# A hybrid retention and sparse-attention layer: pairs of seven in the output projection, a new order in the block sums, idle matmuls ahead, tables spread out, last chunk by token tile

## Chip, core and metric

The kernel runs on one core of a Trainium2 chip. The metric is the device time of one execution in microseconds; the median of three runs of the kernel before is 1888.11 us.

## What is computed

One layer on 256 tokens of width 2048, all in 32-bit floating point: a gated feed-forward network (inner width 5632), a mixer of two halves (retention, and attention over the 64 best keys of an index score), and a second feed-forward network, each added to `x`.

```python
def swiglu(h, w_gate, w_up, w_down):
    return (jax.nn.silu(h @ w_gate) * (h @ w_up)) @ w_down
...
        x = x + 0.5 * swiglu(rmsnorm(x, ffn1_norm[l]), ffn1_w_gate[l], ffn1_w_up[l], ffn1_w_down[l])
        h = rmsnorm(x, mix_norm[l])
        proj = h @ w_in[l]
...
        x = x + jnp.concatenate([ro, ao], axis=-1) @ w_out[l]
        x = x + 0.5 * swiglu(rmsnorm(x, ffn2_norm[l]), ffn2_w_gate[l], ffn2_w_up[l], ffn2_w_down[l])
    return rmsnorm(x, final_norm)
```

## The kernel before

**Products.** Every 32-bit operand is split in two parts, `hi` (rounded by a copy on ScalarE) and `lo` (what is left, a subtraction on VectorE). A product is three matmuls: hi x hi, hi x lo, lo x hi. All have 128 rows of weights and 512 columns.

**Weights.** They come from memory once, 1 MB at a time for two k-tiles of 128 (a "pair"), into `raw` (three buffers), all from SyncE's queue. `split` cuts a pair into pieces of up to 1024 columns and makes `hi` (L269, ScalarE) and `lo` (L275, VectorE) of each; five buffers of each hold them, so a piece is made up to four pieces ahead of its matmuls (two for the first eleven).

**Chunks.** `wide` plans 1024 output columns by two token tiles of 128: 2 x 2 output blocks of 128x512. A pair of kind "C" has eight block products, 24 matmuls (L221). A pair of kind "S" gets the same result from seven products, 21 matmuls, of sums and differences of blocks. It needs four raw sums of the weights on VectorE (`less`, L261), four pieces (512 columns of one product's weights are new), and block sums of the left operand, which `blocks_of` makes (L296 to L306). The products add up in eight PSUM banks: four of output blocks (MAP_B) and four (M1, M5, M6, M7) that `sums_of` combines (L437) once the last pair of seven is done. `UP` names the kinds of the eight pairs of a chunk over the 2048 inputs, `DOWN` those over the hidden inputs. An up chunk is 22 pieces.

**Order.** Each engine runs its instructions in program order. The main loop does, for piece i: the splits up to four pieces ahead, the steps that fall due at i (`after(i, f)`), then the matmuls of i. So a step's instructions on VectorE and ScalarE stand between the `lo` and `hi` of pieces that are four ahead, and wait there for each other.

**A feed-forward network.** It runs in two parts of six and five up chunks, each followed by two down chunks. At the end of an up chunk `hidden` applies the gate (L517, L522). Two pieces or so into the next chunk each half of the result, 256 columns, is transposed on TensorE (`turn`, L529) for the down chunks: where `DOWN` has "S" for the pair it is copied to `b` (L533) and goes through `blocks_of`, where it has "C" it is split plainly (L537, L538). The first up chunk is `PLAIN` and stands in the banks of MAP_A; the others use `UP` and MAP_B. x comes transposed too (`in_xT`), and `x_for` (L288, L324) makes the left operand of each pair of it: pairs 0, 2 and 4 are "S".

**Around the mixer.** `tables` computes angles for the rotary factors in the first network's time on VectorE, steps L617 to L644, with one piece between steps (`yield 1`). The output projection is two chunks of `PLAIN`. `finish` (L581, L583) runs after the last matmul: squares, root of the mean, scaling, four outputs of 512 KB.

Of the kernel before, what the change touches and what calls it, by code (L numbers as in the profile page):

```python
# [19 lines left out]
P = 128  # L20
# [7 lines left out]

PLAIN = "CCCCCCCC"
UP = "SCSCSCCC"  # L30
# [19 lines left out]
def layer(ctx: ExitStack, tc: tile.TileContext, a: dict, out: bass.AP):  # L50
# [32 lines left out]
    MAP_A = {"11": "M7", "12": "M1", "21": "M6", "22": "M5"}  # L83
    MAP_B = {"11": "M2", "12": "M3", "21": "M4", "22": "M8"}
    turn = [0, 0]

    def pair():
        turn[0] += 1
        return [[bank["M1"], bank["M5"]], [bank["M6"], bank["M7"]]][turn[0] % 2]

    def small():
        turn[1] += 1
        return [bank["M2"], bank["M3"], bank["M4"], bank["M8"]][turn[1] % 4]
# [12 lines left out]

    now = [0]
# [66 lines left out]
    def wide(src, plan, left, cmap, x0=False):  # L174

        start = len(pieces)
        seen, last = {}, {}
        s_end = None

        def mm(i, off, a, m):  # L180

            for n, (u, v) in enumerate(((0, 0), (0, 1), (1, 0))):
                st = m not in seen
                seen[m] = 1
                e = [i, off, a, m, u, v, st, False]
                last[m] = e
                pieces[i]["mms"].append(e)

        for p, kind in enumerate(plan):
            loads.append([(0, block(src, 2 * p, 2 * p + 2, 1024))])  # L190
            if x0:
                loads[-1] = [lambda p=p: load_xT(p)] + [(o, loads[-1][0][1][:, o:o + n]) for o, n in
                                                        ([(0, 512), (512, 512), (1024, 1024)] if p == 0 else [(0, 2048)])]
            i = len(pieces)
            if kind == "C":
                tiles = [(0, 1024), (1024, 1024)]
                if x0 and p == 0:
# [6 lines left out]
            if kind == "C":  # L204
                for c in (1, 0):
                    for k in range(2):
                        off = 1024 * (1 - c) + 512 * k
                        j = max(j for j, (o, n) in enumerate(tiles) if o <= off)
                        for t in range(2):
                            mm(i + j, off - tiles[j][0], (t, k), cmap[f"{t + 1}{c + 1}"])  # L210
# [8 lines left out]
    def run_mms(p, hi, lo):  # L219
        for _, off, a, m, u, v, st, sp in p["mms"]:  # L220
            TE.matmul(bank[m], lhsT=p["left"](p["pair"], a)[u], rhs=(hi, lo)[v][:, off:off + 512], start=st, stop=sp)  # L221
# [28 lines left out]
    def split(i):  # L250
# [22 lines left out]
        elif k == 2:  # L273
            less(512, 1536, 1536)
# [17 lines left out]
    def blocks_of(v, sums, alone):  # L292
# [7 lines left out]
        S.activation(alone[:, :2, 0], v[:, :, 0], AF.Copy)  # L300
        S.activation(alone[:, 2, 0], v[:, 1, 1], AF.Copy, scale=-1.0)
        S.activation(sums[:, :, 0], f, AF.Copy)
        V.tensor_tensor(alone[:, :2, 1], v[:, :, 0], alone[:, :2, 0].bitcast(F32), op=OP.subtract)
        V.scalar_tensor_tensor(alone[:, 2, 1], v[:, 1, 1], -1.0, alone[:, 2, 0].bitcast(F32),
                               op0=OP.mult, op1=OP.subtract)
        V.tensor_tensor(sums[:, :, 1], f, sums[:, :, 0].bitcast(F32), op=OP.subtract)  # L306
        return sums, alone

    def s_block(pair, a):
        sums, alone = pair  # L310
        t, i = (sums, int(a[1]) - 1) if a[0] == "S" else (alone, ("A11", "A12", "A22").index(a))
# [97 lines left out]
    def rstd_tok(norm):  # L409
        v = new(tmp, [P, 2], F32, "sum_v", 1)  # L410
        s, k = squares[norm]
        V.tensor_reduce(v, s[:, :, :k[0]], axis=AX.X, op=OP.add)
        V.tensor_scalar(v, v, 1.0 / D, EPS, op0=OP.mult, op1=OP.add)
        r_tok[norm] = new(one, [P, 2], F32, f"r_tok{norm}")
        rsqrt(r_tok[norm], v, 2)
# [41 lines left out]
    def grow(d, scale, at, cmap, norm, done=None):  # L457
# [9 lines left out]
        def ready(c):  # L467
            for t in range(2):
                add_x(t, d, c, bank[cmap[f"{t + 1}{c + 1}"]], scale)

        if s_end is not None:
            after(s_end, early)
        after(half, lambda: ready(1))
# [9 lines left out]
    marks = {}  # L483

    def ffn(which, norm, next_norm, last):
        wgu, wd = a[f"wgu{which}"], [a[f"wd{which}{j}"] for j in range(2)]
        c = 0
        for part, n in enumerate(PARTS):
            hs = {}
            marks[which, part] = len(pieces)  # L490
            for cc in range(n):
                cmap = MAP_A if c == 0 else MAP_B
                start, s_end, half, end = wide(wgu[c], PLAIN if c == 0 else UP, left_of(xg if c == 0 else xs), cmap,
                                               c == 0 and which == 1)
# [638 lines left out]
```

## Time and profile before

| what | us |
|---|---|
| three runs | 1887.54, 1888.11, 1888.51 |
| profiled execution | 1887.65 |
| its span | 1885.8 |
| TensorE busy | 1856.2 (98%) |
| VectorE busy | 1625.8 (86%) |
| ScalarE busy | 1064.9 (56%) |

The span runs from the first to the last instruction that the profiler saw; the 1.85 us around it belong to the execution. Busy time of matmuls overlaps a little, as one is fed while the one before it drains. Rows give the start and the length of an operation in microseconds; behind it, in brackets, stands how long its engine was idle ahead of it, and what ended that.

### The profile page before, as it was taken

What the parts mean: (1) busy time and instruction counts of PE and PEld (TensorE: products, weight loads), DVE (VectorE), ACT (ScalarE), POOL (GpSimd) and SP (SyncE); (2) the same over time, 40 slices, a digit from 0 to 9 for tenths busy, and PEclk for the clock granted to TensorE, in tenths of its full rate; (3) what the DMA queues carried; (4) which work ended last, traced back from release to release, by engine and by line L of the source; (5) the groups of instructions that cost most, each with busy time, mean ns of one, the idle gap of its engine ahead of it and who ended that gap; (6) DMA issues with size and microseconds to landing.
All of it is one profiled execution on the core that took longest, in us unless ns stands there. A gap on an engine that the chain in (4) does not pass through costs nothing.

```text
span 1885.8 us, 22691 instructions
## 1 busy us (share of the span) xinstructions
PE 1856.2 (98%) x8624; PEld 1527.1 (81%) x8624; DVE 1625.8 (86%) x2076; ACT 1064.9 (56%) x1348; POOL 5.3 (0%) x14
## 2 busy tenths in 40 slices
PE   8999999999999999999999999999999999999997
PEld 6788888887888887988888888788888888888886
DVE  7899998889999997789865756799999889999997
ACT  7555655544555555656544555555555455555554
POOL 0000000000000000000000000000000000000000
PEclk9999999999999999999999999999999999999998
DMA  8544555545555454545534444545555555455454
GB/s 323 191 178 180 199 201 221 192 170 178 194 206 203 172 208 156 187 164 211 179 134 173 168 174 178 198 181 191 209 203 180 199 201 200 180 191 210 180 198 159
DMA packets 51309, 359.33 MB, mean 191 GB/s; under 512 B 5856, under 2 KB 5856, under 8 KB 8704
## 3 DMA queue, kind: packets, MB, share of 16 engines
q1 hardware_dynamic: 50400, 355.62, 51.6%
q8 instruction: 67, 1.10, 0.2%
q10 hardware_dynamic: 432, 1.08, 0.2%
q0 software_dynamic: 368, 1.19, 0.2%
q14 instruction: 42, 0.34, 0.1%
HBM read 355.76 MB, written 2.10 MB: 190 GB/s over the span
## 4 chain that ended last, share of the span: by engine, by line
PE 93%; DVE 5%; ACT 1%; issue 1%; DMA 0%; DVEq 0%; ACTq 0%
PE M L221 75%; PE M L145 8%; PE M L147 4%; DVE lo L275 2%; PE M L529 1%; PE M L163 1%; PE M L164 1%; PE M L162 1%; DVE raw L261 1%; DVE x L434 1%; ACT hi L269 1%; PE M L790 0%; DVE e L437 0%; PE M L838 0%; PE M L144 0%
## 5 line engine op out<-in xcount | busy, mean ns | idle before, releaser
L269 ACT ACTIVATE hi<-raw 128x1024 fp32r<-128x1024 f32 (+2 forms) x853 | 843.9, 1008 | 578.8 <-DVE raw L261 356.3
L275 DVE TENSOR_TENSOR lo<-raw,hi 128x1024 fp32r<-128x1024 f32 (+2 forms) x853 | 974.5, 1160 | 152.7 <-ACT hi L269 137.7
L221 PE MATMUL M<-hi,xg 128*128 128x512 f32 x2240 | 738.3, 396 | 1.4 <-DVE e L437 1.4
L221 PE MATMUL M<-hi,mid 128*128 128x512 f32 x1696 | 531.1, 392 | 8.2 <-ACT hi L269 7.8
L221 PEld LDWEIGHTS M<-hi,xg 128*128 128x128 f32 x2240 | 422.6, 189 | 99.5 <-DVE e L437 1.9
L221 PE MATMUL M<-lo,xg 128*128 128x512 f32 x1120 | 444.4, 397 | 2.3 <-DVE lo L275 2.1
L221 PEld LDWEIGHTS M<-hi,mid 128*128 128x128 f32 x1696 | 319.4, 188 | 75.9 <-ACT hi L269 7.8
L221 PE MATMUL M<-lo,mid 128*128 128x512 f32 x848 | 331.5, 391 | 0.1
L261 DVE TENSOR_TENSOR raw<-raw 128x512 f32<-128x512 f32 x368 | 254.7, 692 | 12.4
L221 PEld LDWEIGHTS M<-lo,xg 128*128 128x128 f32 x1120 | 211.4, 189 | 56.7 <-DVE lo L275 8.7
L145 PE MATMUL M<-xg,hi 128*128 128x512 f32 x688 | 245.2, 398 | 1.3 <-DVE xg L289 1.1
L221 PEld LDWEIGHTS M<-lo,mid 128*128 128x128 f32 x848 | 159.8, 188 | 34.6 <-DVE lo L275 1.8
L147 PE MATMUL M<-xg,lo 128*128 128x256 f32 x645 | 182.1, 282 | 0.0
L145 PEld LDWEIGHTS M<-xg,hi 128*128 128x128 f32 x688 | 128.3, 188 | 30.7 <-DVE xg L289 2.2
L221 PE MATMUL M<-hi,ext 128*128 128x512 f32 x360 | 142.4, 395 | 1.9 <-DVE e L522 1.7
L147 PEld LDWEIGHTS M<-xg,lo 128*128 128x128 f32 x645 | 121.4, 188 | 0.8
L221 PEld LDWEIGHTS M<-hi,ext 128*128 128x128 f32 x360 | 67.8, 188 | 18.9 <-DVE e L522 2.6
L221 PE MATMUL M<-lo,ext 128*128 128x512 f32 x180 | 71.2, 395 | 0.1
L437 DVE TENSOR_TENSOR s<-s,M 128x512 f32<-128x512 f32 x96 | 64.1, 682 | 2.2 <-PE M L221 1.2
L517 ACT ACTIVATE s<-s,r_tok 128x512 f32<-128x512 f32 x40 | 27.0, 718 | 54.6 <-DVE s L437 54.6
L221 PEld LDWEIGHTS M<-lo,ext 128*128 128x128 f32 x180 | 33.9, 188 | 8.3 <-DVE lo L275 0.5
L704 ACT ACTIVATE b<-e 64x512 f32<-64x512 f32 (+2 forms) x46 | 28.1, 612 | 19.5 <-DVE e L690 18.9
(173 smaller groups left out, 910.2 us busy)
## 6 DMA issues: line engine op xcount, KB each, us to landing
raw<-in_wgu SPq DMA_DIRECT2D x175, 1024.0 KB, 4.8
raw<-in_wd SPq DMA_DIRECT2D x88, 1024.0 KB, 4.8
raw<-in_w_out SPq DMA_DIRECT2D x16, 1024.0 KB, 4.8
raw<-in_w_iq SPq DMA_DIRECT2D x8, 1024.0 KB, 4.8
raw<-in_w_aq SPq DMA_DIRECT2D x8, 1024.0 KB, 4.8
raw<-in_w_rk SPq DMA_DIRECT2D x8, 1024.0 KB, 4.9
raw<-in_w_rq SPq DMA_DIRECT2D x8, 1024.0 KB, 4.8
raw<-in_w_rv SPq DMA_DIRECT2D x8, 1024.0 KB, 4.8
```

The lines of the kernel that those rows point to most:

```text
L145: TE.matmul(acc, lhsT=hi[:, c:c + P], rhs=r, start=st, stop=sp)
L147: TE.matmul(acc[:, T:], lhsT=lo[:, c:c + P], rhs=r[:, :T], start=False, stop=False)
L162: TE.matmul(o, lhsT=h, rhs=hi[:, i * n:(i + 1) * n], start=st, stop=False)
L163: TE.matmul(o, lhsT=h, rhs=lo[:, i * n:(i + 1) * n], start=False, stop=False)
L164: TE.matmul(o, lhsT=l, rhs=hi[:, i * n:(i + 1) * n], start=False, stop=sp)
L221: TE.matmul(bank[m], lhsT=p["left"](p["pair"], a)[u], rhs=(hi, lo)[v][:, off:off + 512], start=st, stop=sp)
L261: V.tensor_tensor(r[:, o:o + 512], r[:, a:a + 512], r[:, b:b + 512], op=OP.subtract)
L269: S.activation(hi[:, :p["n"]], raw, AF.Copy)
L275: V.tensor_tensor(lo[:, :p["n"]], raw, hi[:, :p["n"]].bitcast(F32), op=OP.subtract)
L437: V.tensor_tensor(o, a, b, op=OP.add)
L517: S.activation(s, g, AF.Silu, scale=r_tok[norm][:, t:t + 1])
L704: S.activation(b[p0:p0 + w], q[p1:p1 + w], AF.Copy)
```

## The change

- The output projection's first chunk uses `UP` (three pairs of seven), its second stays plain and uses the banks of OTHER. `left_pair` makes a left operand of either kind, for the mixer's results too.
- `UP` is now "CSCSCSCC", and `ORDER` lays the pairs out so that a chunk still runs S C S C S C C C. The pairs of x that are "S" are 1, 3 and 5; x's first pair is split plainly.
- `blocks_of` issues ScalarE's copy of the four sums ahead of that of the blocks that stand alone; the latter are four (of x three), in one copy and one subtraction; the sign of one block moves into the raw sums.
- The plain chunk of each network stands in the banks SUM, and its results are copied or gated from there.
- Fourteen idle matmuls of 128 columns stand ahead of all others.
- `tables` has three pieces between steps.
- In the last chunk the matmuls of the last two pairs are ordered by token tile; `finish` does all of a tile before the other, in pieces of 512 columns, with eight outputs of 256 KB; `gain_first` comes at the last three pieces instead of the last eight.
- The transposes of x around the second network use other banks (`turn_early`, `turn_late`).

```diff
+UP = "CSCSCSCC"
+ORDER = (1, 0, 3, 2, 5, 4, 6, 7)
 PLAIN = "CCCCCCCC"
-UP = "SCSCSCCC"
...
-    MAP_A = {"11": "M7", "12": "M1", "21": "M6", "22": "M5"}
-    MAP_B = {"11": "M2", "12": "M3", "21": "M4", "22": "M8"}
+    SUM = {"11": "M2", "12": "M3", "21": "M4", "22": "M8"}
+    OTHER = {"11": "M7", "12": "M1", "21": "M6", "22": "M5"}
...
+                            if tail and p >= len(plan) - 2:
+                                ending[t].append((i + j, off - tiles[j][0], p, (t, k), sums[f"{t + 1}{c + 1}"]))
+                                continue
+                            mm(i + j, off - tiles[j][0], (t, k), sums[f"{t + 1}{c + 1}"])
...
+        ending[1].sort(key=lambda e: e[4], reverse=True)
+        for t in range(2):
+            for i, off, p, a, m in ending[t]:
+                mm(i, off, a, m, i if t == 0 else len(pieces) - 1)
...
-            less(512, 1536, 1536)
+            less(1536, 512, 1536)
...
-        S.activation(alone[:, :2, 0], v[:, :, 0], AF.Copy)
-        S.activation(alone[:, 2, 0], v[:, 1, 1], AF.Copy, scale=-1.0)
+        vt = v.rearrange("p k t n -> p t k n")
         S.activation(sums[:, :, 0], f, AF.Copy)
-        V.tensor_tensor(alone[:, :2, 1], v[:, :, 0], alone[:, :2, 0].bitcast(F32), op=OP.subtract)
-        V.scalar_tensor_tensor(alone[:, 2, 1], v[:, 1, 1], -1.0, alone[:, 2, 0].bitcast(F32),
-                               op0=OP.mult, op1=OP.subtract)
+        if alone.shape[1] == 4:
+            a4 = alone.rearrange("p (t k) h n -> p t k h n", t=2)
+            S.activation(a4[:, :, :, 0], vt, AF.Copy)
+            V.tensor_tensor(a4[:, :, :, 1], vt, a4[:, :, :, 0].bitcast(F32), op=OP.subtract)
+        else:
+            for o, w in ((slice(0, 2), vt[:, 0]), (slice(2, 3), vt[:, 1, 1:2])):
+                S.activation(alone[:, o, 0], w, AF.Copy)
+                V.tensor_tensor(alone[:, o, 1], w, alone[:, o, 0].bitcast(F32), op=OP.subtract)
         V.tensor_tensor(sums[:, :, 1], f, sums[:, :, 0].bitcast(F32), op=OP.subtract)
...
+    def left_pair(kind, v, in_psum=True):
+
+        if kind == "S":
+            if in_psum:
+                f = half_k("b")
+                S.activation(f, v, AF.Copy)
+                v = f
+            return blocks_of(v, big(F32R, (P, 4, 2, P)), big(F32R, (P, 4, 2, P)))
+        t = big(F32R, (P, 2, 512))
+        S.activation(t[:, :, :T], v, AF.Copy)
+        V.tensor_tensor(t[:, :, T:], v, t[:, :, :T].bitcast(F32), op=OP.subtract)
+        return t
...
+                def ups(u=u, plain=plain):
                     for b in ("12", "22"):
-                        if b in u:
-                            full(b)
-
-                def hidden(u=u, full=full, cc=cc, part=part, hs=hs, cmap=cmap):
-                    ht, sil = [], []
+                        if plain:
+                            u[b] = new(tmp, [P, W], F32, "e", 3)
+                            S.activation(u[b], bank[SUM[b]], AF.Copy)
+                        else:
+                            tt(u[b], u[b], bank[SUM[b]])
...
+                    for b in ("11", "21"):
+                        t = int(b[0]) - 1
+                        if plain:
+                            u[b] = new(tmp, [P, W], F32, "s")
+                        else:
+                            tt(u[b], u[b], bank[SUM[b]])
+                        S.activation(u[b], bank[SUM[b]] if plain else u[b], AF.Silu, scale=r_tok[norm][:, t:t + 1])
+                    ht = [u["12"], u["22"]]
...
+            rstd_tok(3, slice(t, t + 1))
             r = r_tok[3][:, t:t + 1]
-            xs = [x[t][:, halves(c, 1024)] for c in range(2)]
-            S.activation(xs[0], xs[0], AF.Copy, scale=r)
-            V.scalar_tensor_tensor(xs[1], xs[1], r, last_gain[1], op0=OP.mult, op1=OP.mult)
-            for c in range(2):
-                nc.sync.dma_start(out[t][:, halves(c, 1024)], xs[c])
+            for c in range(4):
+                xs = x[t][:, halves(c)]
+                if c < 2:
+                    S.activation(xs, xs, AF.Copy, scale=r)
+                else:
+                    V.scalar_tensor_tensor(xs, xs, r, last_gain[1][:, halves(c - 2)], op0=OP.mult, op1=OP.mult)
+                nc.sync.dma_start(out[t][:, halves(c)], xs)
...
+    for _ in range(14):
+        TE.matmul(bank["M1"][:, :P], lhsT=ones, rhs=ones, start=True, stop=True)
...
-        yield 1
+        yield 3
...
-        cmap = (MAP_A, MAP_B)[d]
-        at = wide(a["w_out"][d], PLAIN, left_of(mix_in), cmap)
-        grow(d, 1.0, at, cmap, 2)
+        sums = OTHER if d else SUM
+        at = wide(a["w_out"][d], PLAIN if d else UP, left_of(mix_in), order=None if d else ORDER, sums=sums)
+        grow(d, 1.0, at, 2, sums=sums)
...
-    after(end - 8, gain_first)
+    after(end - 3, gain_first)
```

A turn for a pair of seven (523 us in the trace of before): ScalarE, from the copy out of PSUM (`b`) to the next weight piece's `hi`. `sq` holds the four sums, the `mid` after it is the sums' parts, that with `b` as its source the blocks that stand alone. Before:

```order
L533 ACTIVATE b_1448<-M_5_76 128x512
L300 ACTIVATE mid_1451<-b_1448 128x2x128
L301 ACTIVATE mid_1451<-b_1448 128x128
L302 ACTIVATE mid_1450<-sq_1452 128x4x128
L537 ACTIVATE mid_1467<-M_7_78 128x2x256
L269 ACTIVATE hi_1470<-raw_1381 128x1024
```

Two copies of alone blocks stand ahead of the copy of the sums. After, the same place on ScalarE:

```order
L329 ACTIVATE b_1460<-M_5_76 128x512
L312 ACTIVATE mid_1462<-sq_1464 128x4x128
L315 ACTIVATE mid_1463<-b_1460 128x4x128
L333 ACTIVATE mid_1477<-M_7_78 128x2x256
L280 ACTIVATE hi_1480<-raw_1393 128x1024
```

The copy of the sums now stands first, that of the alone blocks behind it. VectorE in the same turn, before:

```order
L299 TENSOR_TENSOR sq_1452<-b_1448,sq_1452 128x128
L303 TENSOR_TENSOR mid_1451<-b_1448,mid_1451 128x2x128
L304 SCALAR_TENSOR_TENSOR mid_1451<-b_1448,mid_1451 128x128
L306 TENSOR_TENSOR mid_1450<-sq_1452,mid_1450 128x4x128
L538 TENSOR_TENSOR mid_1467<-M_7_78,mid_1467 128x2x256
L275 TENSOR_TENSOR lo_1471<-raw_1381,hi_1470 128x1024
```

The residues of the alone blocks read what L300 and L301 wrote, that of the sums what L302 wrote. After, on VectorE:

```order
L310 TENSOR_TENSOR sq_1464<-b_1460,sq_1464 128x128
L316 TENSOR_TENSOR mid_1463<-b_1460,mid_1463 128x4x128
L321 TENSOR_TENSOR mid_1462<-sq_1464,mid_1462 128x4x128
L334 TENSOR_TENSOR mid_1477<-M_7_78,mid_1477 128x2x256
L286 TENSOR_TENSOR lo_1481<-raw_1393,hi_1480 128x1024
```

The alone residue is one operation, still first, and reads what ScalarE's second copy wrote. The program's start on ScalarE: `e` is a transposed pair of x, `xg` and `mid` its plain parts, `b` the copy for the sums, `ext` the alone blocks of x. Before:

```order
L288 ACTIVATE mid_114<-e_101,gains_72 128x256 x2
L324 ACTIVATE b_119<-e_101,gains_72 128x256 x2
L300 ACTIVATE ext_123<-b_119 128x2x128
L301 ACTIVATE ext_123<-b_119 128x128
L302 ACTIVATE xg_29_122<-sq_124 128x4x128
L269 ACTIVATE hi_135<-raw_100 128x512
L269 ACTIVATE hi_139<-raw_100 128x512
L269 ACTIVATE hi_143<-raw_100 128x1024
L288 ACTIVATE xg_40_157<-e_107,gains_72 128x256 x2
L269 ACTIVATE hi_162<-raw_106 128x1024
```

After:

```order
L299 ACTIVATE xg_27_128<-e_115,gains_72 128x256 x2
L280 ACTIVATE hi_133<-raw_114 128x512
L280 ACTIVATE hi_137<-raw_114 128x512
L280 ACTIVATE hi_141<-raw_114 128x1024
L299 ACTIVATE mid_155<-e_121,gains_72 128x256 x2
L357 ACTIVATE b_160<-e_121,gains_72 128x256 x2
L312 ACTIVATE xg_38_163<-sq_165 128x4x128
L319 ACTIVATE ext_164<-b_160 128x2x128
L319 ACTIVATE ext_164<-b_160 128x128
L280 ACTIVATE hi_176<-raw_120 128x1024
```

The block sums moved from ahead of the first pair's weights to ahead of the second pair's.

## Rows read from the trace of the kernel before

**Rows 1.** Part 1 of the page: busy time, share of the span, instructions.

```profile
PE 1856.2 (98%) x8624; PEld 1527.1 (81%) x8624; DVE 1625.8 (86%) x2076; ACT 1064.9 (56%) x1348; POOL 5.3 (0%) x14
```

**Rows 2.** Waits of TensorE: total us, times, longest.

```profile
PE M L221 <- ACT hi L269: 7.8, 1, 7.8
PE M L221 <- DVE lo L275: 2.1, 2, 1.8
```

**Rows 3.** Timeline of VectorE, 515 to 560 us: start, length, operation.

```profile
523.74 0.29 DVE L299 TENSOR_TENSOR sq<-b,sq 128x128 f32<-128x128 f32 x1
...
524.73 0.69 DVE L306 TENSOR_TENSOR mid<-sq,mid 128x512 fp32r<-128x512 f32 x1 [0.16 <-ACT mid L302]
525.34 0.68 DVE L538 TENSOR_TENSOR mid<-M,mid 128x512 fp32r<-128x512 f32 x1
526.16 1.23 DVE L275 TENSOR_TENSOR lo<-raw,hi 128x1024 fp32r<-128x1024 f32 x1
...
538.93 1.42 DVE L522 SCALAR_TENSOR_TENSOR e<-e,r_tok,s 128x512 f32<-128x512 f32 x2 [0.20 <-ACT s L517]
540.49 3.50 DVE L275 TENSOR_TENSOR lo<-raw,hi 128x1024 fp32r<-128x1024 f32 x3
```

**Rows 4.** Timeline of ScalarE, 515 to 560 us.

```profile
524.06 0.63 ACT L302 ACTIVATE mid<-sq 128x512 fp32r<-128x512 f32 x1 [0.44 <-DVE sq L299]
524.60 0.58 ACT L537 ACTIVATE mid<-M 128x512 fp32r<-128x512 f32 x1
```

**Rows 5.** Timeline of TensorE, 540.5 to 543.2 us.

```profile
541.21 0.40 PE L221 MATMUL M<-hi,ext 128*128 128x512 f32 x1
541.44 0.40 PE L221 MATMUL M<-hi,xg 128*128 128x512 f32 x1
541.77 0.50 PE L221 MATMUL M<-lo,xg 128*128 128x512 f32 x1
```

**Rows 6.** Groups by line and form: count, busy us, mean ns, idle ahead.

```profile
L306 DVE TENSOR_TENSOR mid<-sq,mid 128x512 fp32r<-128x512 f32 x16 | 11.1, 693 | 2.6 <-ACT mid L302 2.6
```

**Rows 7.** Timeline of TensorE, 54 to 57 us.

```profile
54.51 0.39 PE L221 MATMUL M<-hi,xg 128*128 128x512 f32 x1
55.76 0.50 PE L221 MATMUL M<-hi,ext 128*128 128x512 f32 x1 [0.86 <-DVE e L522]
```

**Rows 8.** Stretches: length, busy us (instructions) of PE, PEld, DVE, ACT, POOL; clock; DMA.

```profile
410.00:453.60 43.60, 40.01 (x162) 30.84 (x161) 42.91 (x58) 18.93 (x22) 0.00 (x0) 0.96 0.47 161
...
497.20:540.80 43.60, 43.60 (x193) 35.08 (x192) 41.49 (x53) 25.18 (x31) 0.00 (x0) 1.00 0.52 192
```

**Rows 9.** Stretches in the output projection, the same columns.

```profile
1080.00:1100.00 20.00, 20.00 (x90) 16.57 (x89) 9.42 (x9) 8.26 (x8) 0.00 (x0) 1.00 0.50 167
1100.00:1120.00 20.00, 20.00 (x90) 16.57 (x89) 11.94 (x12) 10.06 (x14) 0.00 (x0) 1.00 0.57 206
```

**Rows 10.** Groups by line: the first and the last of the tables' twelve.

```profile
L617 DVE CAST mid<-mid 128x256 f32<-128x256 int32 x1 | 0.3, 286 | 0.0
...
L644 DVE TENSOR_SCALAR mid<-mid 128x1024 f32<-128x1024 f32 x1 | 0.7, 683 | 0.0
```

**Rows 11.** Timelines of the start.

```profile
9.24 1.05 PE L221 MATMUL M<-hi,mid 128*128 128x512 f32 x2
9.63 0.89 ACT L288 ACTIVATE xg<-e,gains 128x256 fp32r<-128x256 f32 x2
...
11.86 2.01 ACT L269 ACTIVATE hi<-raw 128x1024 fp32r<-128x1024 f32 x2 [1.33 <-DMA raw<-in_wgu]
...
21.49 0.39 PE L221 MATMUL M<-hi,mid 128*128 128x512 f32 x1
```

**Rows 12.** Timeline of the end.

```profile
1873.44 0.39 PE L221 MATMUL M<-hi,mid 128*128 128x512 f32 x1
...
1876.83 2.48 DVE L581 SCALAR_TENSOR_TENSOR x<-x,r_tok,mid 128x1024 f32<-128x1024 f32 x2
1878.00 2.89 SPq L583 DMA_DIRECT2D out_T<-x  x4
```

More of the change, by code (lines that the diff above doesn't have):

```diff
@@ L172, in layer, with wide, mm @@
         (3, 0, "A22", "M4"))
[L174 removed]
+    def wide(src, plan, left, x0=False, tail=False, order=None, sums=SUM):
         start = len(pieces)
         seen, last = {}, {}
+        ending = [[], []]
         s_end = None
[L180 removed]
+        def mm(i, off, a, m, at=None, p=None):
             for n, (u, v) in enumerate(((0, 0), (0, 1), (1, 0))):
@@ L217, in wide, with run_mms @@
         return start, s_end, len(pieces) - 1, len(pieces)
-    def run_mms(p, hi, lo):
-        for _, off, a, m, u, v, st, sp in p["mms"]:
-            TE.matmul(bank[m], lhsT=p["left"](p["pair"], a)[u], rhs=(hi, lo)[v][:, off:off + 512], start=st, stop=sp)
+    def run_mms(p):
+        for i, off, (pair, a), m, u, v, st, sp in p["mms"]:
+            TE.matmul(bank[m], lhsT=p["left"](pair, a)[u], rhs=split_of[i][v][:, off:off + 512], start=st, stop=sp)
     def block(src, l0, l1, width):
@@ L465, in early, with ready @@
                 add_x(int(b[0]) - 1, d, int(b[1]) - 1, u[b], scale)
-        def ready(c):
-            for t in range(2):
-                add_x(t, d, c, bank[cmap[f"{t + 1}{c + 1}"]], scale)
+        def ready(c, ts=(0, 1)):
+            for t in ts:
+                add_x(t, d, c, bank[sums[f"{t + 1}{c + 1}"]], scale)
         if s_end is not None:
             after(s_end, early)
+        if final:
+            after(end, lambda: finish(ready))
+            return
         after(half, lambda: ready(1))
@@ L491, in ffn @@
             for cc in range(n):
-                cmap = MAP_A if c == 0 else MAP_B
-                start, s_end, half, end = wide(wgu[c], PLAIN if c == 0 else UP, left_of(xg if c == 0 else xs), cmap,
-                                               c == 0 and which == 1)
+                plain = c == 0
+                start, s_end, half, end = wide(wgu[c], PLAIN if plain else UP, left_of(xg if plain else xs),
+                                               plain and which == 1, order=None if plain else ORDER)
@@ L555, in ffn @@
                 if final:
-                    after(end, finish)
-                elif part == 1 and not last:
-                    if d == 0:
-                        turns = list(range(4))
-                    else:
-                        for i, m in enumerate(("M1", "M5", "M6", "M7")):
-                            after(s_end + 2 + i, lambda i=i, m=m: turn_x(i, next_norm, m))
-                        turn_rest(end, next_norm)
-        return end
-    def turn_rest(end, norm):
-        for s, c, m in ((0, 6, "M3"), (0, 7, "M8"), (1, 4, "M2"), (1, 5, "M4")):
-            after(end + s, lambda c=c, m=m: turn_x(c, norm, m))
@@ L571, in finish, with turn_early, turn_late @@
-    def finish():
-        for c in (1, 0):
-            for t in range(2):
+                    pass
+                elif part == 1 and not last and d == 1:
+                    turn_early(s_end, next_norm)
+                    turn_late(end, next_norm, ("M2", "M4", "M3", "M8"))
+        return end
+    def turn_early(s_end, norm):
+        for i, m in enumerate(("M1", "M5", "M6", "M7")):
+            after(s_end + 2 + i, lambda i=i, m=m: turn_x(i, norm, m))
+    def turn_late(end, norm, banks):
+        for i, s in ((2, 0), (3, 0), (0, 1), (1, 1)):
+            after(end + s, lambda i=i: turn_x(4 + i, norm, banks[i]))
```

129 lines of the change are left out of this document (56 added, 73 removed).

## Prediction

> **What bounds the kernel now.** First the busy shares [rows 1]: TensorE is busy 98% of the span, VectorE 86%, ScalarE 56%. So a microsecond is only won where TensorE computes less, waits less or runs at its full clock, and only lost where another engine makes it wait. Next the table of TensorE's waits: only 2.1 us in all stand against VectorE's `lo` (the rest of a weight piece) [rows 2], which looks as if VectorE had slack. The timelines say otherwise at one kind of place. Take the 128x512 output block of an up chunk that is transposed for a pair of seven (an "S turn"). ScalarE copies it out of PSUM to `b`; VectorE makes four block sums (the last is L299), then the residues of the blocks that stand alone (L303, L304), of the sums (L306), of the second block of the turn (L538), and only then `lo` of the next weight piece, at 526.16 [rows 3]. On ScalarE it waits 0.16 us [rows 3]. There are 16 such turns (L306 x16) [rows 6]. From there VectorE works on without a pause but one of 0.20 us, ahead of L522 [rows 3], up to the run of three `lo` that starts at 540.49 [rows 3]. The first of them, 1.23 long, is ready at 541.72, and the matmul that reads it starts at 541.77: 0.33 us after the one ahead of it, where 0.23 is usual [rows 5]. It is the first piece of the chunk's first plain pair. Setting the end of each `lo` against its first matmul through the whole trace gives the same behind all 16 turns: there that piece is ready only 0.05 us ahead, while after a turn of two plain pairs it is 1.2 us ahead, and other pieces 1.8 to 8 us. So a delay that enters VectorE's stream at an S turn reaches TensorE 15 us later.
>
> **The change part by part.** The sum is made against the profiled execution, 1887.65 us (span 1885.8), 0.46 below the median 1888.11.
>
> *Order inside an S turn.* Before, ScalarE copied the alone blocks (L300, L301) while VectorE was still adding, so VectorE went on from the last sum (L299, to 524.03) to their residues without a pause [rows 3]; the copy of the sums (L302, 524.06 to 524.69) [rows 4] ran beside it. After, ScalarE copies the sums first and then all four alone blocks, and VectorE takes the alone residue first, behind ScalarE's second copy. Priced with the rows: L312 like L302 from 524.06, then the alone copy, a 128x512 one like L302 too, 0.54 after it (the distance L302 to L537) [rows 4], so 524.60 to 525.23. VectorE idles from 524.03 to about 525.26. Then come L316 (the alone residue in one operation), L321 and L334, each 0.61 after the other as L538 came after L306 [rows 3], so `lo` starts at 527.09. It started at 526.16: +0.93 us a turn; ScalarE's `hi` for it, two copies of 0.54 later than in [rows 4], is no later than that. What is queued behind the waiting VectorE is that `lo`, the combinations of the seven products, raw sums, and at the end of the row the piece with 0.05 us to spare; TensorE waits for that. 16 x (0.93 - 0.05) = 14.1, and up to 16 x 0.93 = 14.9 where the 0.10 us of wait [rows 5] was there already; I take 0.92 each, **+14.7**, near the upper end because [rows 5] shows a wait. The lower bound is 0, if VectorE made it good on the way.
>
> *Output projection.* Its first chunk becomes three pairs of seven: 3 x 3 matmuls less, 9 x 0.23 [rows 5] = **-2.1**. VectorE gets twelve raw sums and about eight combinations at 0.69 (like L306 [rows 6]) and three times 1.5 pieces of `lo` at 1.23 [rows 3]: 19.3 us. In the 40 us of the two rows of this stage VectorE is free 10.58 + 8.06 us [rows 9], 20.5 in a chunk of 44. It just fits; cover gone, the excess is TensorE's: 0 to +1.5, taken **+0.3**. The two mix pairs' block sums fall into a stage whose VectorE is as free; they go with this.
>
> *Banks of the plain chunks.* At 54.51 and 1206.22 TensorE waits for VectorE to read M1 before it can start the first pair of the next chunk: 55.76 - 54.51 = 1.25, less 0.23, is 1.02 [rows 7]. The plain chunk now stands in the banks of the other set, and the next chunk starts in free ones: 2 x 1.02 = **-2.0**, nothing to -2.0. The copies that this adds (512 columns on ScalarE) lie beside matmuls.
>
> *Tables.* In 410 to 453.6 us TensorE did 162 matmuls where a like stretch has 193 [rows 8]: 31 x 0.23 = 7.1 us lost, of which the clock's mean of 0.96 is 1.7. VectorE's inserted work, twelve lines from L617 to L644, is 13.9 us [rows 10]. It is now spread three times as wide, over two chunks. But VectorE has 2.1 us free in 43.6 of a usual chunk, 0.7 in this one [rows 8], and most of it is the waits inside the turns. So only about 1.4 us more find room, and I add a third of the clock's 1.7: **-2.0**. Ends: -7.1 if all is hidden, +1 if two steps land just before an S turn's `lo`.
>
> *Clock and start.* TensorE starts at 7.85 [rows 2]. Two matmuls take 1.05 us at first [rows 11] where 0.63 (0.40 + 0.23) is usual [rows 5]: 0.2 us more for each. The clock is at its lower level of 1.2 GHz, as TensorE had done nothing before; the granted clock has no record that early. The first two pairs, 48 matmuls of 0.23, last from 7.85 to 21.49 [rows 2, 11], 13.6 us instead of 11.0, so some 12 are slow. Fourteen idle matmuls now run while TensorE waits for data, and could take up to 12 x 0.2 = 2.4 us off. But x's second pair is now one of seven, and its sums' copies stand on ScalarE ahead of that pair's weights. From 9.63 [rows 11]: 0.89 for x's pair, again 0.89 for `b`, four sums on VectorE to 12.75, copies (0.6 and 0.7) to 13.9, `hi` to 14.93, `lo` to 16.2, 24 matmuls of 0.23: pair 2 at about 21.5. Before it was 21.49 [rows 11]. So a faster first pair only waits longer for the second: **0**. Ends: -2.8 if ScalarE came to the second pair's weights at 11.86 as before [rows 11], +1.9 if the pause brings the low clock back.
>
> The Trainium skill ("TensorE: Matmul & The Clock Gate", Part 1) says that the throttled clock is the default state and that activity releases it. It speaks for the idle matmuls, and no run here has had any; by it alone the sum would be 2.4 us lower, which is a rival below.
>
> *End.* Before, after the last matmul at 1873.44: additions, squares, root, scaling of 1024 columns from 1876.83 (2.48 for two), outputs from 1878.00, end of the program's span 1885.8 [rows 12]. After, token tile 0 is done while tile 1's 24 matmuls (5.5 us) run. Tile 1: its two additions and squares as before, root near 1877.9 since its small steps still come one by one, scaling in 512 pieces to 1879.3, last issue about 1880. One of two megabytes is then still to go, and the end comes to about 1883.5: **-2.3** (-1.1 to -3.5).
>
> *Sum:* 14.7 - 2.1 + 0.3 - 2.0 - 2.0 + 0 - 2.3 = +6.6, so 1894.2 against the profiled 1887.65, and 1894.7 as a median. The case's own range, by the ends of tables, start and end, is 1889 to 1899.
>
> **The rivals.**
> 1. *VectorE takes the turn's delay up.* TensorE then pays nothing at the 16 turns and the sum is -8.1: 1880.0, faster. For it: TensorE waits only 2.1 us for `lo` in all [rows 2], and pieces run four ahead. Against it: the 0.05 to 0.1 us ahead, at all 16. It decides when a turn costs TensorE under 0.27 us; break-even is 0.5.
> 2. *Tables and start come off whole.* The remaining 5.1 of the tables and 2.8 at the start: 1894.7 - 7.9 = 1886.8, no change. For it: spreading triples the room in count of pieces. Against: VectorE's free time [rows 8] and ScalarE's order at the start.
> 3. *The idle matmuls pay whole.* 1894.7 - 2.4 = 1892.3, slower. It needs the second pair's weights to be ready sooner than I laid out.
> 4. *The clock falls.* A pause at the start or in the tables brings a stretch of half clock, as 1.7 us were lost that way [rows 8]; twice that, 3.4: 1898.1, slower.
>
> A change that doesn't do what it says is not among them: the order of instructions shows each part done.
>
> **How the numbers follow.** Forecast 0.60 (slower). Rival 1 0.13 (faster), rival 2 0.11 (same), rival 3 0.10 and rival 4 0.06 (slower). A measurement can tell 0.2%, 3.8 us: faster is below 1884.3, slower above 1891.9. Faster 0.13, same 0.11, slower 0.76. The range leaves out rival 1 and the far ends: 1884 to 1899.5.
>
> **What would show it.** Right: VectorE idle about 1.2 us ahead of L316, sixteen times, and TensorE's waits for `lo` near 15 us in all; no wait at the two plain-chunk boundaries; pair 2 of the first chunk at 21 to 22 us; last output issued about 1880 plus what was lost before. Wrong: waits for `lo` still near 2 us (rival 1); 190 or more matmuls in the tables' first chunk (rival 2); pair 2 at 19 us (rival 3); a clock below 0.9 in a stretch that showed 1.00 (rival 4).

## The result: slower by 0.55%

| kernel | median us | runs, us | ratio to the kernel before (95%) |
|---|---|---|---|
| before | 1888.01 | 1887.54 to 1888.51, 6 runs | |
| changed | 1898.06 | 1896.84 to 1900.09, 6 runs | 1.0055 (1.0042 to 1.0068) |

The change costs 10 us, where 6.6 were forecast. Its profiled execution took 1896.84 us (span 1895.1), the fastest of its six runs; on why the others took 1 to 3 us more there is only an estimate, further down.

The page's first part and the table of TensorE's waits (total us, times, longest), to be set beside [rows 1, 2]:

```profile
PE 1862.9 (98%) x8643; PEld 1525.0 (80%) x8643; DVE 1646.2 (87%) x2109; ACT 1072.9 (57%) x1351; POOL 5.3 (0%) x14
```

```profile
PE M L232 <- DVE lo L286: 7.1, 19, 1.0
PE M L560 <- DVE s L471: 2.6, 1, 2.6
PE M L232 <- DVE e L986: 1.7, 1, 1.7
```

Before, TensorE waited for `lo` twice, now it does 19 times (15 at the S turns clear of the tables, two at the start, two in the tables' stretch). TensorE has 9 matmuls less of 512 columns, and 14 small ones more (28 records).

Now the same S turn as in [rows 3, 4], first VectorE, then ScalarE:

```profile
524.90 0.29 DVE L310 TENSOR_TENSOR sq<-b,sq 128x128 f32<-128x128 f32 x1
526.41 0.69 DVE L316 TENSOR_TENSOR mid<-b,mid 128x512 fp32r<-128x512 f32 x1 [1.22 <-ACT mid L315]
527.02 0.68 DVE L321 TENSOR_TENSOR mid<-sq,mid 128x512 fp32r<-128x512 f32 x1
527.63 0.68 DVE L334 TENSOR_TENSOR mid<-M,mid 128x512 fp32r<-128x512 f32 x1
528.23 1.22 DVE L286 TENSOR_TENSOR lo<-raw,hi 128x1024 fp32r<-128x1024 f32 x1
...
540.99 1.42 DVE L553 SCALAR_TENSOR_TENSOR e<-e,r_tok,s 128x512 f32<-128x512 f32 x2 [0.20 <-ACT s L550]
542.55 3.50 DVE L286 TENSOR_TENSOR lo<-raw,hi 128x1024 fp32r<-128x1024 f32 x3
```

```profile
525.23 0.63 ACT L312 ACTIVATE mid<-sq 128x512 fp32r<-128x512 f32 x1 [1.09 <-DVE sq L310]
525.77 0.62 ACT L315 ACTIVATE mid<-b 128x512 fp32r<-128x512 f32 x1
```

From the last sum to `lo` it is 528.23 - 524.90 = 3.33 us; before it was 526.16 - 523.74 = 2.42. The difference is 0.91. The distance from this `lo` to L553 is 12.76 us, before it was 12.77: nothing on the way is made up. What waits at the end of it, in TensorE's timeline:

```profile
539.72 0.40 PE L232 MATMUL M<-hi,xg 128*128 128x512 f32 x1
540.25 0.50 PE L232 MATMUL M<-hi,ext 128*128 128x512 f32 x1
...
543.15 0.40 PE L232 MATMUL M<-hi,xg 128*128 128x512 f32 x1
543.83 0.50 PE L232 MATMUL M<-lo,xg 128*128 128x512 f32 x1 [0.28 <-DVE lo L286]
```

The first matmul that reads the `lo` of 542.55 starts 0.68 us after the one ahead of it (0.23 is usual, 0.33 before, [rows 5]), and 3.4 us earlier another step has 0.53. Set against the trace before, matmul by matmul, these two steps are 0.35 and 0.30 longer and two others 0.11 each: 0.87 for this turn. The brackets show little of this: a matmul is 0.40 long but a new one starts each 0.23, so of a delay the first 0.17 are no idle time, and the 0.13 left at 540.25 has no bracket at all. The waits' table adds the brackets up, 0.28 to 0.35 a turn, which is why it has 7.1 us (2.6 of them at the start and in the tables) for a loss of 14 at the turns.

The start of each chunk on TensorE, set against the same chunk of the kernel before, gives the account. Worked out from the starts of the first matmuls of all chunks of both traces:

| place | forecast us | traces us |
|---|---|---|
| start, to x's third pair (21.49 before, 20.92 after) | 0 | -0.6 |
| plain chunk to next chunk, twice | -2.0 | -1.0 and -1.05 |
| 16 S turns (15 clear of the tables: 13.3, 0.75 to 1.04 each) | +14.7 | +14.2 |
| tables, over three up chunks, without their turn | -2.0 | -1.5 |
| output projection's first chunk | -1.8 | +1.4 |
| end, last matmul's start to the span's end (12.40 to 10.35) | -2.3 | -2.05 |
| small steps elsewhere | 0 | -0.2 |
| span (1885.85 to 1895.07) | +6.6 | +9.2 |

Below, a chunk's step is how much longer it takes on TensorE, from its first matmul to that of the next chunk, than in the kernel before.

### The profile page after: what moved, and what is told of

Same layout as the page of the kernel before. It is cut to its first block, busy times and chain, and to the rows that moved or that the text cites. A ratio compares the mean times of both kernels' runs of the same rounds, so it can differ in the third digit from the quotient of the medians.

```text
span 1895.1 us, 22782 instructions
## 1 busy us (share of the span) xinstructions
PE 1862.9 (98%) x8643; PEld 1525.0 (80%) x8643; DVE 1646.2 (87%) x2109; ACT 1072.9 (57%) x1351; POOL 5.3 (0%) x14
## 4 chain that ended last, share of the span: by engine, by line
PE 75%; DVE 19%; ACT 3%; issue 2%; DMA 0%; SPq 0%; DVEq 0%; ACTq 0%
PE M L232 58%; DVE lo L286 8%; PE M L146 8%; PE M L148 4%; DVE raw L272 3%; DVE e L471 2%; ACT hi L280 1%; DVE s L471 1%; PE M L164 1%; PE M L165 1%; PE M L163 1%; DVE x L468 1%; PE M L560 1%; DVE mid L316 1%; ACT mid L315 1%
## 5 line engine op out<-in xcount | busy, mean ns | idle before, releaser
L272 DVE TENSOR_TENSOR raw<-raw 128x512 f32<-128x512 f32 x380 | 262.9, 692 | 12.7
L471 DVE TENSOR_TENSOR e<-s,M 128x512 f32<-128x512 f32 x58 | 39.6, 684 | 1.0
```

The costliest lines, as they stand in the source:

```text
L272: V.tensor_tensor(r[:, o:o + 512], r[:, a:a + 512], r[:, b:b + 512], op=OP.subtract)
L471: V.tensor_tensor(o, a, b, op=OP.add)
```

## Experiments

### The order inside the S turns

The theory (T) is the forecast's; the rival (R) is that VectorE makes a turn's delay good, and that the 10 us come from elsewhere. Three kernels tell them apart. The first undoes this one part in the changed kernel:

```diff
-        S.activation(sums[:, :, 0], f, AF.Copy)
         if alone.shape[1] == 4:
             a4 = alone.rearrange("p (t k) h n -> p t k h n", t=2)
             S.activation(a4[:, :, :, 0], vt, AF.Copy)
             V.tensor_tensor(a4[:, :, :, 1], vt, a4[:, :, :, 0].bitcast(F32), op=OP.subtract)
+            S.activation(sums[:, :, 0], f, AF.Copy)
...
         else:
+            S.activation(sums[:, :, 0], f, AF.Copy)
```

> The changed kernel, but in the block sums ScalarE copies the blocks that stand alone first and the sums second, as before the change. Theory T (the order inside the S turns costs TensorE about 0.9 us at each of 16 turns): 1898.1 - 14.4 = 1883.7 us, and each S turn's step against the kernel before falls from 0.75 to 1.0 us to about zero. Rival R (the loss comes from the added work on VectorE and the waits in the output projection, the turns' delay is made up on the way): 1896 to 1898.

Measured: 1883.84 us (1881.76 to 1884.70, 9 runs), ratio to before 0.9972 (0.9962 to 0.9982): 14.2 us less than the changed kernel, and faster than both. That it meets the expected 14.4 so closely is in part luck. Between the two traces the spans differ by 12.5: the turns give 14.3 and the output projection 1.1 more, but e1's start is 2.1 later (a stretch at half clock, below) and its end 0.8 longer. The steps at the turns are 0.00, -0.01, -0.01, -0.14 in the first four chunks. VectorE's timeline of the turn:

```profile
522.46 0.29 DVE L310 TENSOR_TENSOR sq<-b,sq 128x128 f32<-128x128 f32 x1
522.67 0.68 DVE L315 TENSOR_TENSOR mid<-b,mid 128x512 fp32r<-128x512 f32 x1
523.45 0.69 DVE L322 TENSOR_TENSOR mid<-sq,mid 128x512 fp32r<-128x512 f32 x1
524.06 0.68 DVE L335 TENSOR_TENSOR mid<-M,mid 128x512 fp32r<-128x512 f32 x1
524.89 1.23 DVE L286 TENSOR_TENSOR lo<-raw,hi 128x1024 fp32r<-128x1024 f32 x1
```

The 1.22 us of idle time are gone, and from the last sum to `lo` it is 2.43 us, as before the change. The second kernel puts the part alone into the kernel before:

```diff
+        S.activation(sums[:, :, 0], f, AF.Copy)
         S.activation(alone[:, :2, 0], v[:, :, 0], AF.Copy)
         S.activation(alone[:, 2, 0], v[:, 1, 1], AF.Copy, scale=-1.0)
-        S.activation(sums[:, :, 0], f, AF.Copy)
```

> The kernel before, with one edit: ScalarE copies the sums ahead of the two copies of the alone blocks. Theory T: VectorE starts the alone residue at about 525.06 instead of 523.95, and lo comes 0.78 us later a turn, 16 x 0.78 = 12.5: 1900.5 us. Rival R: within 2 us of 1888.0.

Measured: 1898.62 us (4 runs), ratio 1.0053 (1.0038 to 1.0068). One move of one line in the kernel before costs as much as the whole change. By the traces about 0.6 us of it falls on each turn (0.47 to 0.69, 9.3 in all), less than the 0.78 expected. VectorE's timeline of the turn:

```profile
527.49 0.29 DVE L299 TENSOR_TENSOR sq<-b,sq 128x128 f32<-128x128 f32 x1
528.78 0.42 DVE L303 TENSOR_TENSOR mid<-b,mid 128x256 fp32r<-128x256 f32 x1 [1.00 <-ACT mid L301]
...
530.53 1.22 DVE L275 TENSOR_TENSOR lo<-raw,hi 128x1024 fp32r<-128x1024 f32 x1
```

It waits 1.00 us at L303, but no longer at L306 (0.16 before, [rows 3]), which the expectation had left out: from the last sum to `lo` it is 3.04 us.

The third is a dose between: ScalarE as changed, but VectorE takes the residues in the order in which the copies end.

```diff
             S.activation(a4[:, :, :, 0], vt, AF.Copy)
+            V.tensor_tensor(sums[:, :, 1], f, sums[:, :, 0].bitcast(F32), op=OP.subtract)
             V.tensor_tensor(a4[:, :, :, 1], vt, a4[:, :, :, 0].bitcast(F32), op=OP.subtract)
+            return sums, alone
```

> The changed kernel, with VectorE taking the residue of the sums first and that of the alone blocks second, in the order in which ScalarE's copies end; ScalarE as in the changed kernel. Theory T, as a dose between the two: VectorE waits until 524.73 instead of 525.26 (times of the turn at 523), so 0.53 us less a turn, 16 x 0.53 = 8.5: 1889.6 us. Rival R: 1897 to 1898.

Measured: 1891.44 us (1890.58 to 1893.05, 10 runs), ratio 1.0017 (1.0008 to 1.0026): 6.6 us less than the changed kernel, where 8.5 were expected. VectorE's timeline of the turn:

```profile
523.71 0.29 DVE L310 TENSOR_TENSOR sq<-b,sq 128x128 f32<-128x128 f32 x1
524.70 0.69 DVE L316 TENSOR_TENSOR mid<-sq,mid 128x512 fp32r<-128x512 f32 x1 [0.70 <-ACT mid L312]
...
526.65 1.22 DVE L286 TENSOR_TENSOR lo<-raw,hi 128x1024 fp32r<-128x1024 f32 x1
```

VectorE's wait is 0.52 us shorter, as expected, but `lo` comes only 0.39 sooner: ScalarE makes `hi` of that piece from 525.57 to about 526.6, and `lo` now waits for it.

The five kernels side by side, from the last sum's start to that of `lo` on VectorE (the turn shown), and the step of TensorE at a usual turn:

| kernel | last sum to `lo`, us | more than before | step on TensorE |
|---|---|---|---|
| before | 2.42 | | |
| e1, alone blocks first | 2.43 | 0.01 | 0.00 |
| e3, residues in the copies' order | 2.94 | 0.52 | 0.52 |
| e2, the move alone | 3.04 | 0.62 | 0.61 |
| changed | 3.33 | 0.91 | 0.89 |

At the turn shown itself the chunk step is 0.75, 0.47 and 0.36 in the changed kernel, e2 and e3 and -0.15 in e1, so set against e1 it is 0.90, 0.62 and 0.51. What `lo` loses TensorE loses, one for one. Theory T holds, and R falls: nothing is made good.

### The start

Taken out of the changed kernel: the fourteen idle matmuls.

> The changed kernel without the fourteen idle matmuls. Theory S (the second pair's weights, behind its sums' copies on ScalarE, set the pace of the start, so a warm first pair only waits longer): the first pair of the second chunk starts at 54.2 to 54.7 us as in the changed kernel (54.17), total 1898.1 to 1898.6. Rival (the idle matmuls pay whole): 2.4 us more, 56.6 us and 1900.5.

Measured: 1897.27 us (4 runs), beside 1898.06, which these runs do not tell apart. In the traces x's third pair starts at 21.59 without and at 20.92 with them, 0.7 us. TensorE's timelines, first the changed kernel:

```profile
12.88 0.40 PE L232 MATMUL M<-hi,xg 128*128 128x512 f32 x1
14.31 0.50 PE L232 MATMUL M<-hi,mid 128*128 128x512 f32 x1 [1.02 <-ACT hi L280]
15.57 0.50 PE L232 MATMUL M<-lo,mid 128*128 128x512 f32 x1 [0.76 <-DVE lo L286]
```

and without the idle matmuls:

```profile
14.76 0.40 PE L232 MATMUL M<-hi,xg 128*128 128x512 f32 x1
14.99 0.48 PE L232 MATMUL M<-hi,mid 128*128 128x512 f32 x1
16.22 0.50 PE L232 MATMUL M<-lo,mid 128*128 128x512 f32 x1 [0.75 <-DVE lo L286]
```

In the changed kernel the first pair ends 1.9 us earlier and then waits for the second pair's `hi` and `lo`, as the forecast had it. Nor are the 0.7 us the work of the idle matmuls: they are already there on ScalarE, where the first pair's last weights come from memory that much later. Changed kernel, e4, and e3, which has the idle matmuls:

```profile
8.09 1.06 ACT L280 ACTIVATE hi<-raw 128x1024 fp32r<-128x1024 f32 x1 [0.92 <-DMA raw<-in_wgu]
8.75 1.06 ACT L280 ACTIVATE hi<-raw 128x1024 fp32r<-128x1024 f32 x1 [1.03 <-DMA raw<-in_wgu]
8.68 1.06 ACT L280 ACTIVATE hi<-raw 128x1024 fp32r<-128x1024 f32 x1 [1.65 <-DMA raw<-in_wgu]
```

In e3, with the full clock at its start too, the third pair starts at 21.50. So what the idle matmuls win can't be told from nothing. With them the first pair's matmuls come 0.23 apart, but for their waits, without them they are 0.42 apart at first. The Trainium skill ("TensorE: Matmul & The Clock Gate", Part 1) has activity release the throttle, and the traces agree. The rival that the idle matmuls pay whole falls all the same, on ScalarE's order: the second pair's weights are not ready sooner.

If that order decides, making the second pair's block sums behind its weights should help. Tried on the kernel of e1:

```diff
             split_x(c, norm, xT, big(F32R, (P, 2, 512)))
+            if norm == 0 and c == 1:
+                later.append(lambda: s_of_x(c, norm, xT))
+                return
             s_of_x(c, norm, xT)
...
         split_of[i] = (hi, lo)
+        if later and p["off"]:
+            later.pop()()
```

> The kernel of e1 (1883.84 us) with the block sums of x's second pair made behind that pair's weights in the first chunk. Theory S (those copies on ScalarE set the pace of the start): the two waits at the second pair (1.02 + 0.76 us) fall to under 1 in all, and with no such pause no stretch of half clock follows, as it did in e1's look (17.1 to 20.5 us): 1.0 to 3 us less, 1881 to 1883. Rival (the second pair's weights arrive from memory no earlier): 1883.8.

Measured: 1882.31 us (1881.48 to 1882.72, 6 runs) beside e1's 1883.84, in the expected range; but the kernel before, run beside each, differs by 0.6 (1887.90 and 1888.46), and the ratios to it, 0.9969 (0.9956 to 0.9981) and 0.9972, do not tell the two apart. The trace shows the part: the second pair now follows the first without a wait, only `lo` is late, and the third pair starts at 19.98 instead of 20.76 to 21.50 (e7, changed, e3):

```profile
13.16 0.39 PE L232 MATMUL M<-hi,xg 128*128 128x512 f32 x1
13.39 0.47 PE L232 MATMUL M<-hi,mid 128*128 128x512 f32 x1
14.62 0.50 PE L232 MATMUL M<-lo,mid 128*128 128x512 f32 x1 [0.76 <-DVE lo L286]
```

In e1's own trace the pause at the second pair was followed by a stretch at the lower clock level, in the changed kernel's trace, with the same pause, it was not. Stretches of e1 and of the changed kernel (length, busy time of PE, PEld, DVE, ACT, POOL with their instructions, granted clock, DMA):

```profile
13.30:17.10 3.80, 2.02 (x8) 1.11 (x7) 3.52 (x6) 3.80 (x7) 0.00 (x0) 1.00 0.99 409
17.10:20.50 3.40, 3.40 (x10) 2.66 (x9) 3.40 (x6) 2.83 (x6) 0.00 (x0) 0.50 0.79 266
```

```profile
12.88:17.10 4.22, 2.44 (x10) 1.46 (x9) 3.96 (x7) 4.22 (x8) 0.00 (x0) 1.00 0.95 387
17.10:20.50 3.40, 3.40 (x17) 2.82 (x16) 3.40 (x6) 2.40 (x5) 0.00 (x0) 1.00 0.81 282
```

Ten matmuls at half the clock (1.2 GHz) against 17: 1.7 us. So behind the second pair's wait, itself 1.8 us of idle time, some executions lose 1.7 more. The sums' later place is no cure for that: e10, with the same start, waits 1.26 and 0.75 us for the first pair's weights, and its clock is at half from 11.9 to 15.3.

### Tables

Back to one piece between the steps, in the changed kernel:

```diff
-        yield 3
+        yield 1
```

> The changed kernel with one piece between the steps of the tables, as before the change. By the changed kernel's trace the tables' stretch (the second up chunk of the first network's second half part until the fourth) stands at -4.41 + 1.48 + 2.28 us against the kernel before, of which two S turns are 1.8, so the spreading is worth 2.4: 1898.1 + 2.4 = 1900.5. Rival (spreading only moves the loss to the next chunks): 1898.

Measured: 1900.46 us (1899.93 to 1900.74, 4 runs), 2.4 more, which is what was expected; but the account behind the 2.4 was wrong. Only one S turn falls into those chunks, not two, so the traces give 1.5 for the spreading: this kernel stands exactly as before the change there (steps 0.00 and 0.00, then 0.79 with the turn), where the changed kernel gains 4.41 in the first chunk and loses 1.48 and 2.28 in the next two. The rest of the 2.4 is not shown. This kernel's trace has a stretch at half clock at the start, as e1's, and its third pair starts 2.0 us later than in the changed kernel; the runs without a trace may or may not have one.

A stretch at half clock in the tables is another matter. The changed kernel has none there, e4 and e7 have one of 3.4 us behind the wait at 474 us. They take 1.6 and 1.5 us longer over the second of the three chunks, and over all three the steps are -0.65, -0.62 and -0.70: nothing is left of it. In e5, with e1's order, it is the same (-1.65 beside -1.48). What limits these chunks is VectorE, and TensorE would have waited for it anyway; that reason is argued from the row below, not tested.

What the spreading leaves, in the changed kernel's row for the chunk behind [rows 8]:

```profile
444.24:491.75 47.51, 43.88 (x193) 35.20 (x192) 45.50 (x58) 24.04 (x28) 0.00 (x0) 1.00 0.48 177
```

43.6 us of matmuls take 47.5; VectorE works 45.5 of them.

### The output projection

The forecast gave it -1.8, and it took +1.4. Two waits stand in TensorE's timeline at its beginning:

```profile
1078.84 0.50 PE L232 MATMUL M<-hi,mid 128*128 128x512 f32 x1 [0.82 <-DVE e L719]
...
1083.56 0.50 PE L232 MATMUL M<-hi,mid 128*128 128x512 f32 x1 [1.69 <-DVE e L986]
```

Their steps, 1.09 and 2.08 us, are 2.7 more than the usual, of the 3.4 by which the chunk misses the nine matmuls' gain of 2.1. L986 reads the last mixer result out of bank M8, which the second pair of this chunk needs. VectorE comes to it late: ahead of it stand the raw sums of the first pair of seven and, in this kernel, a block sum's 1.22 us of idle time. VectorE's rows:

```profile
1069.32 0.69 DVE L316 TENSOR_TENSOR mid<-e,mid 128x512 fp32r<-128x512 f32 x1 [1.22 <-ACT mid L315]
...
1070.53 2.14 DVE L272 TENSOR_TENSOR raw<-raw 128x512 f32<-128x512 f32 x3
...
1082.63 0.87 DVE L986 SCALAR_TENSOR_TENSOR e<-M,gains,s 128x256 f32<-128x256 f32 x2
```

With e1's order the first wait is gone, the second still 1.65, and the chunk's step is +0.3, so 1.1 belonged to the order of the copies. For the rest a new theory (W): the wait goes if a plain pair comes first and the last result takes another bank. Tried on e1's kernel:

```diff
+ORDER_OUT = (0, 2, 1, 4, 3, 6, 5, 7)
-        ps = small() if c < 3 else bank["M8"]
+        ps = small() if c < 3 else bank["M7"]
-        at = wide(a["w_out"][d], PLAIN if d else UP, left_of(mix_in), order=None if d else ORDER, sums=sums)
+        at = wide(a["w_out"][d], PLAIN if d else UP, left_of(mix_in), order=None if d else ORDER_OUT, sums=sums)
```

> The kernel of e1 (alone blocks copied first, 1883.84 us) with the output projection's first chunk in the order C C S C S C S C instead of S C S C S C C C, and the last mixer result transposed in bank M7 instead of M8. Theory W (the 1.65 us that TensorE waits there for L987 is VectorE's queue of raw sums, which stands ahead of the last mixer result's gate): the wait goes, the chunk's step against the kernel before falls from +0.27 to -1.4 to -2.0 us, 1881.8 to 1882.2. Rival (VectorE's 42 us of work in the chunk's 45 is too much in any order): a wait for lo later in the chunk takes its place, step -0.5 to +1, 1883 to 1885.

Measured: 1886.20 us (1884.80 to 1887.39, 10 runs), 2.4 more than e1. Both totals were wrong. The chunk's step is -2.03, all of the nine matmuls' gain: the wait went, as theory W said, and within this chunk VectorE's room does suffice. But the next chunk lost 4.72:

```profile
1115.63 0.80 PE L233 MATMUL M<-hi,mid 128*128 128x512 f32 x1 [3.04 <-DVE e L473]
```

With a pair of seven as the last but one, the shared sums are still being combined when the second chunk wants their banks, and TensorE starts again in a stretch at half clock (a mean of 0.79 over 1112 to 1120). So the sevens need plain pairs ahead of them, for the mixer, and behind them, for the banks. The order C S C S C S C C has both; it was tried on e8's kernel, with e5's bank:

```diff
+ORDER_OUT = (0, 1, 2, 3, 4, 5, 6, 7)
```

> The kernel of e8 (1882.31 us) with the output projection's first chunk in the order C S C S C S C C and the last mixer result transposed in bank M7. Theory W as put after e5 (the wait for the mixer's result goes when a plain pair comes first, and the wait of 3.0 us for L473 at the second chunk goes when two plain pairs stand behind the last pair of seven): the chunk's step against the kernel before is -1.2 to -2.0 us, as it was -2.03 in e5, and the next chunk's about 0 instead of +4.72: 1880.0 to 1880.9. Rival (VectorE's work in that chunk fits in no order): step 0 or more, 1882.3 or more.

Measured: 1880.43 us (1879.71 to 1881.34, 4 runs), ratio to before 0.9960 (0.9945 to 0.9975), the fastest but for e10, from which it can't be told. The chunk's step is -1.27, the next one's 0.00; of the wait 0.53 is left:

```profile
1075.90 0.47 PE L233 MATMUL M<-hi,mid 128*128 128x512 f32 x1 [0.53 <-DVE e L993]
```

### Tables over all chunks

On e9's kernel, seven pieces between the steps instead of three.

> The kernel of e9 with seven pieces between the steps of the tables instead of three, so that they reach over all five up chunks. Theory V (what the tables cost is their work less VectorE's free time in the chunks they lie in, about 2 us a chunk): three more chunks hide up to 6 us; in e8's trace the stretch still cost about 5 us, so 2 to 4 us less than e9, 1877 to 1879. Rival (VectorE's free time lies in waits inside the turns and takes no work in): no change against e9.

Measured: 1880.26 us (1879.15 to 1881.34, 4 runs): no change, so theory V falls. Set against the kernel before, the second of the chunks, which loses 1.56 in e9, gains 2.64, and the chunks behind it lose 2.20, 0.79, 1.24 and 0.54, each with an S turn in it. Over all of them e10 is 0.7 better than e9 by the traces, where 2 to 4 were expected. VectorE is idle 1.94 us in a usual chunk of e9 (the one from 533.7), 1.04 of that in gaps under 0.15 us between its operations; in e10's chunks with an S turn and steps of the tables 0.98 to 1.41 us are left. So at most about 1 us a chunk takes work in. The rival has the total right, though its reason is only part of it.

### The end

The end of the kernel before, in the changed kernel (both tiles together, four outputs, matmuls and `gain_first` in the old places).

> The changed kernel with the end of the kernel before (both tiles together, four outputs of 512 KB). By the traces the time from the last matmul's start to the span's end fell from 12.36 to 10.38 us, so 1898.1 + 2.0 = 1900.1. Rival (the last matmuls' new order costs TensorE what the end gains): 1898.

Measured: 1900.69 us (1898.38 to 1900.83, 4 runs), 2.6 more; by the traces 12.39 us from the last matmul's start instead of 10.35, so 2.0. Rows of the changed kernel's end, beside [rows 12]:

```profile
1884.72 0.39 PE L232 MATMUL M<-hi,mid 128*128 128x512 f32 x1
```

```profile
1888.87 1.42 DVE L609 SCALAR_TENSOR_TENSOR x<-x,r_tok,mid 128x512 f32<-128x512 f32 x2
```

```profile
1884.75 6.81 SPq L610 DMA_DIRECT2D out_T<-x  x8
```

The scaling starts 4.15 us after the last matmul instead of 3.39, and yet the end comes 2 us sooner, since the first megabyte was issued from 1884.75, while TensorE was finishing. The 2.0 belong to this trace: in e1, e3 and e8, with the same end but without some or all of the turns' delay, it is 1.2 to 1.3 (VectorE comes to the second tile's additions 1.45 us after the last matmul's start in e1 and 0.61 in the changed kernel); in e9 it is 2.1 again. Why it is one or the other stays open.

## Right and wrong, point by point

- **S turns: right, in mechanism and size.** +0.93 us was read from the rows for VectorE's `lo`, 0.91 came, and 0.89 reached TensorE, 15 us later, at each turn. Rival 1, that it would be taken up, fell by e1, e2 and e3. One sign held, VectorE's wait of 1.22 us ahead of L316 (19 times, as three pairs of the mixer have it too). The other was wrong: waits for `lo` near 15 us were announced, and the table has 7.1. The table counts idle time behind a matmul's modelled end; the loss has to be read from starts. The distance given for pieces elsewhere, 1.8 to 8 us, is too large at its lower end: at the third piece of the second pair of seven it is 1.1 in most up chunks. The 0.05 at the turns is right for all 16, and it is what counts.
- **Output projection: the term that failed**, by 3.2 us. The other terms' misses of +0.5, -0.5, -0.6, +0.3 and -0.2 nearly cancel, so the sum misses the span by 2.6. It weighed VectorE's work against its free time over the whole chunk (19.3 in 20.5) and found that it fits. It does, as e5's -2.03 shows. What it didn't ask is where the work falls: the raw sums of the first pair go ahead of the mixer's last result in VectorE's order, and the second pair's bank waits for that. The range of 0 to +1.5 for it was too narrow; 3.4 us came, 2.7 of them in the two waits.
- **Banks of the plain chunks: right**, 1.0 and 1.05 for 1.02 each, read from the traces; no run undoes this part.
- **Tables: right in sign, 1.5 for 2.0.** The part added for the clock isn't borne out: e4, e5 and e7 show that a stretch at half clock behind the wait at 474 us costs nothing over the three chunks. That VectorE's free time is mostly waits in the turns was only half right: in the chunk of before from 492.87, 2.11 us, 0.55 is such a wait and 1.01 are gaps under 0.15. Rival 2 fell, but the sign set for it nearly came: the first of the chunks has 189 matmuls in 43.6 us, as it lost nothing, and the loss moved to the next two.
- **Start: 0 was forecast, -0.6 came.** The chain on ScalarE was right (second pair's `hi` ready at 14.3, `lo` at 15.6, forecast 14.9 and 16.2). The 0.6 is the first pair's weights arriving from memory that much earlier than in e3 and e4, where the third pair starts 0.01 and 0.09 behind the kernel before; the idle matmuls show no gain of their own, and rival 3 with its 2.4 falls.
- **The clock, rival 4:** not in the changed kernel's trace, which has the full clock from 4.70 us until after the last matmul, but in others of nearly the same kernel, at the start (e1, e5, e6, e10) and behind the tables' wait at 474 us (e4, e5, e7). The rival's total, 1898.1, is the measured median to 0.1; that is luck, as the profiled execution is 9.2 us above the kernel before without any such stretch.
- **End: right**, -2.0 for -2.3 (1.2 in some of the other kernels).

The median is 1.2 above the profiled execution, where 0.46 was added. Of the six runs two took 1900.1 us, at a mean clock of 0.996 instead of 0.998. A stretch of half clock at the start costs 1.7 us, half of that difference by this estimate; those runs have no trace, and what the rest is stays open.

## What to carry to other kernels

Where two engines hand blocks to each other in a fixed order, issue on the first engine what the second can use while it is still making the other input; a copy that could have run beside four additions cost 0.9 us a time when it came behind them. Look for the place where a piece is ready only just before its use, and count its repetitions: total idle time, busy shares and the waits' table all hid it. And room over a whole chunk says nothing on an operation early in it: ask what will stand ahead of it in its engine's order.

## What was not expected of the hardware

- A stretch of TensorE at its lower clock level follows a pause in one execution and not in another: after the pauses of 1.4 and 1.3 us at the second pair there was one in e1 (17.1 to 20.5 us) and none in the changed kernel; after the wait of 2.65 us at 474 there was one in e4 (granted clock 0.63 over 478 to 482) and none in the changed kernel (1.00). At the start such a stretch costs 1.7 us that nothing makes good, so single executions differ by that; in the tables, where VectorE is behind, its 1.5 us are gone one chunk later.
- Ahead of a matmul of 512 columns the bracket leaves out the first 0.17 us of a wait, since these matmuls are 0.40 long and 0.23 apart: a step of 0.68 has a bracket of 0.28.
- When the first weights come from memory varies by 0.8 us from execution to execution: ScalarE's work on the first pair's last piece starts at 7.89 (e7), 8.09 (changed) and 8.68 us (e3), with the same program up to there.
